# One layer of a hybrid decoder in split single precision: W_down as seven half-size block products

## The chip, the cores and the metric

The kernel runs on one core of a Trainium2 chip. The metric is the device time of one execution in microseconds (us). Beside the times there is a hardware profile of one execution: what each engine did and when. The engines are PE (TensorE, matrix products), ACT (ScalarE), DVE (VectorE), POOL (GpSimd) and SP (SyncE, which here only starts DMAs).

## The reference, cut to what matters

```python
# x: (512, 1024) tokens by features; p: (512, 256); one layer
h = rms_norm(x, g_pre_mix)
q, k, v, cb, cc, cu, ga, gc = split(h @ w_in)             # 8 heads of 64; conv and gates
o = stick_breaking_attention(q, k, v)                     # strictly causal
y_conv = (cb * causal_conv3(cc * cu)) @ w_conv_out
x = x + rms_norm((sigmoid(ga) * (o @ w_attn_out) + sigmoid(gc) * y_conv) @ w_o, g_post_mix)
f = square(relu(rms_norm(x, g_pre_mlp) @ w_up)) @ w_down  # w_up 1024x4096, w_down 4096x1024
x = x + rms_norm(f, g_post_mlp)
x = x + sigmoid(rms_norm(x, g_ple) @ w_ple_gate) * (p @ w_ple_proj)
```

The change is about the second product in the line for f: 512 tokens by 4096 hidden features times W_down.

## The kernel before

Every matrix product is done in split single precision. A value is split into a high part, which ACT copies out in the shorter format float32r, and a low part, which DVE gets as the difference (`split`). `mm3` then issues three matmuls: high by high, high by low, low by high. One matmul is a 128 x 128 stationary tile by 128 x 512 moving columns into a PSUM bank. There are eight banks of 512 columns.

The stages run in this order: norm of x, transposes and v; attention and convolution; the gated mix; W_o with its norms; p @ W_ple_proj; W_up with relu squared; W_down with its norms; the gated per-layer embedding. The order on PE and on SP is the order of the code (`manual_schedule`). The order on ACT, DVE and POOL is made by the framework's scheduler when the kernel is built. Each engine, and each queue of DMAs, works strictly in its order, so one instruction that waits holds all those behind it.

Weights come through `weights` (called by `wcols` and `wrow`): a DMA of 512 KB into one of four `raw` buffers, then two splits of half a tile into a `whi` and a `wlo` tile. The pool `wts` holds five of each. A third pool, `big`, has 16 tiles of 8 KB a partition for activations.

Attention goes over four pairs of heads (the loop over j). For each pair PE makes the scores of head a and of head b (`scores`), then two convolution products (`conv_u`, `conv_b`), then the transposes of head a's weights (`wtrans(wa)`), the next query product, the transposes of head b's weights (`wtrans(wb)`), the next key product, the products with v (`av`, twice), and the next `conv_c`. Inside `scores`, ACT makes two sigmoids, beta and keep; POOL cuts each at the diagonal with `affine_select` (eight of these instructions a head); DVE does a running product over keep (line 304) and a multiplication (line 305), four of each a head. After `wtrans`, DVE makes the low parts `wtl` which `av` reads.

W_down is called as `rows(FF // P, acts, w_down, 4, chain2)`: for each of 32 row blocks k, four token tiles t by two column halves, three matmuls each, accumulating in all eight banks. The last four k are done token tile by token tile, and `chain2(t)` follows each: `residual` squares the sums (ACT), gets the reciprocal root (a `pow` on POOL, line 119, writing `rs`), scales and adds to x (DVE, lines 468 and 469), squares again, `pow` again, and scales (line 475). The result hn2[t] is transposed on PE (`transposed2`, line 127) two token tiles later and split into h3, which the last stage multiplies with W_ple_gate. W_o has the same ending with `chain1`, hn1 and h2.

## Time and profile before

| | |
|---|---|
| times of three runs | 768.0, 768.71, 769.34 us (median 768.71) |
| span of the profiled execution, first to last instruction | 764.4 us |
| PE busy | 756.4 us, 3528 matmuls |
| DVE busy | 388.1 us |
| ACT busy | 301.7 us |
| POOL busy | 49.8 us |
| HBM read, written | 74.99 MB, 2.10 MB |
| granted TensorE clock | 1.000 |

The profiled execution's own time is known as its span; the times of the runs are of other executions, and their median is 4.3 us above the span. A row of the profile names the line of the kernel, the engine, the operation, and out<-in by the names of the tiles; "x236" is a count, and then come busy microseconds, the mean of one in nanoseconds, and the engine's idle time ahead of these instructions with what ended it. Matmuls overlap, so the pitch from one start to the next is shorter than the duration of one. Rows of the timeline start with the start in us and the length in us.

### The profile page before, as it was taken

To read this page: it belongs to the slowest core of one execution; us is meant where nothing else is said; L and a number is where in the kernel's file an instruction comes from. 1 tells how busy PE (TensorE), PEld (TensorE's weight loads), DVE (VectorE), ACT (ScalarE), POOL (GpSimd) and SP (SyncE) were. 2 spreads that over 40 slices of the span, in tenths; PEclk is the share of its full clock that TensorE was granted. 3 is DMA by queue.
4 is the path that set the end of the run, shared out by engine and by line. 5 is a ranking of instruction groups with operands and counts; after the bars stand their busy time and mean duration, and the time that the engine had idled before them with its cause. 6 is when DMAs were issued, how large, how long until landed. Compare 5 with 4: busy or idle time off the path is not lost.

```text
span 764.4 us, 9131 instructions
## 1 busy us (share of the span) xinstructions
PE 756.4 (99%) x3528; PEld 631.9 (83%) x3528; DVE 388.1 (51%) x643; ACT 301.7 (39%) x586; POOL 49.8 (7%) x91
## 2 busy tenths in 40 slices
PE   8999999999999999999999999999999999999997
PEld 6888888888888888888988888888888888888886
DVE  5759797976434345348433333333652543234742
ACT  7654645554333334228323232323631433222511
POOL 1013314040000000001000000000000000000100
PEclk9999999999999999999999999999999999999999
DMA  9512130414634623211633333332323442410011
GB/s 303 163 58 83 55 111 29 131 31 115 193 111 130 200 87 106 83 56 34 187 86 108 86 107 89 104 101 94 110 84 109 138 165 87 161 56 1 0 56 55
DMA packets 91106, 77.66 MB, mean 102 GB/s; under 512 B 2580, under 2 KB 81208, under 8 KB 91064
## 3 DMA queue, kind: packets, MB, share of 16 engines
q1 hardware_dynamic: 91064, 77.10, 32.9%
q8 instruction: 27, 0.44, 0.2%
q14 instruction: 15, 0.12, 0.1%
HBM read 74.99 MB, written 2.10 MB: 101 GB/s over the span
## 4 chain that ended last, share of the span: by engine, by line
PE 98%; ACT 1%; DMA 1%; DVE 0%; issue 0%; SPq 0%; POOL 0%; ACTq 0%
PE ps L83 31%; PE ps L85 31%; PE ps L84 31%; PE ps L334 1%; PE ps L320 1%; PE ps L127 1%; PE ps L293 1%; PE ps L292 1%; DMA xin<-in_x_dram 1%; ACT h1h L197 0%; PE ps L188 0%; ACT vh L61 0%; ACT junk L111 0%; PE ps L433 0%; POOL rs L119 0%
## 5 line engine op out<-in xcount | busy, mean ns | idle before, releaser
L62 DVE TENSOR_TENSOR wlo<-raw,whi 128x512 fp32r<-128x512 f32 x236 | 158.2, 686 | 253.2 <-ACT whi L61 253.0
L61 ACT CAST whi<-raw 128x512 fp32r<-128x512 f32 x236 | 141.5, 623 | 328.1 <-PE ps L84 174.8
L83 PE MATMUL ps<-h1h,whi 128*128 128x512 f32 x288 | 113.0, 392 | 0.0
L85 PE MATMUL ps<-h1h,wlo 128*128 128x512 f32 x288 | 112.3, 390 | 0.0
L84 PE MATMUL ps<-h1l,whi 128*128 128x512 f32 x288 | 112.2, 390 | 0.0
L83 PE MATMUL ps<-h2h,whi 128*128 128x512 f32 (+1 forms) x272 | 102.5, 377 | 0.0
L84 PE MATMUL ps<-h2l,whi 128*128 128x512 f32 (+1 forms) x272 | 102.4, 377 | 0.0
L85 PE MATMUL ps<-h2h,wlo 128*128 128x512 f32 (+1 forms) x272 | 102.4, 377 | 0.0
L83 PE MATMUL ps<-whi,ah 128*128 128x512 f32 x256 | 99.7, 389 | 0.0
L85 PE MATMUL ps<-whi,al 128*128 128x512 f32 x256 | 99.6, 389 | 0.0
L84 PE MATMUL ps<-wlo,ah 128*128 128x512 f32 x256 | 99.6, 389 | 0.0
L85 PEld LDWEIGHTS ps<-h1h,wlo 128*128 128x128 f32 x288 | 54.1, 188 | 11.2
L84 PEld LDWEIGHTS ps<-h1l,whi 128*128 128x128 f32 x288 | 54.1, 188 | 10.9
L83 PEld LDWEIGHTS ps<-h1h,whi 128*128 128x128 f32 x288 | 54.1, 188 | 10.8
L85 PEld LDWEIGHTS ps<-h2h,wlo 128*128 128x128 f32 x272 | 51.2, 188 | 9.4
L84 PEld LDWEIGHTS ps<-h2l,whi 128*128 128x128 f32 x272 | 51.2, 188 | 9.4
L83 PEld LDWEIGHTS ps<-h2h,whi 128*128 128x128 f32 x272 | 51.2, 188 | 9.3
L84 PEld LDWEIGHTS ps<-wlo,ah 128*128 128x128 f32 x256 | 48.1, 188 | 10.0
L85 PEld LDWEIGHTS ps<-whi,al 128*128 128x128 f32 x256 | 48.1, 188 | 9.9
L83 PEld LDWEIGHTS ps<-whi,ah 128*128 128x128 f32 x256 | 48.1, 188 | 9.9
L119 POOL TENSOR_TENSOR rs<-ms,mhalf 128x1 f32<-128x1 f32 x20 | 11.8, 588 | 565.7 <-DVE ms L117 513.5
L301 POOL TENSOR_SCALAR_AFFINE_SELECT beta<-beta 128x128 f32<-128x128 f32 x32 | 26.3, 833 | 107.9 <-ACT beta L295 107.7
(133 smaller groups left out, 1000.3 us busy)
## 6 DMA issues: line engine op xcount, KB each, us to landing
raw<-in_w_in_dram SPq DMA_DIRECT2D x36, 512.0 KB, 3.8
raw<-in_w_up_dram SPq DMA_DIRECT2D x32, 512.0 KB, 4.0
raw<-in_w_down_dram SPq DMA_DIRECT2D x32, 512.0 KB, 3.3
raw<-in_w_o_dram SPq DMA_DIRECT2D x8, 512.0 KB, 3.4
raw<-in_w_ple_gate_dram SPq DMA_DIRECT2D x8, 512.0 KB, 3.3
xin<-in_x_dram SPq DMA_DIRECT2D x4, 512.0 KB, 9.5
vr<-in_w_in_dram SPq DMA_DIRECT2D x4, 512.0 KB, 7.5
raw<-in_w_conv_out_dram SPq DMA_DIRECT2D x8, 256.0 KB, 2.8
```

Of the source, the lines that this page charges most:

```text
L61: nc.scalar.copy(hi, src)
L62: nc.vector.tensor_tensor(lo, src, hi.bitcast(F32), op=ALU.subtract)
L83: nc.tensor.matmul(ps, lh, rh, start=start, stop=False)
L84: nc.tensor.matmul(ps, lh, rl, start=False, stop=False)
L85: nc.tensor.matmul(ps, ll, rh, start=False, stop=stop)
L119: nc.gpsimd.tensor_tensor(r, m, mhalf, op=ALU.pow)
L127: nc.tensor.transpose(ps[:, i * P:(i + 1) * P], hn[g][:, i * P:(i + 1) * P], ident)
L292: nc.tensor.matmul(ps[:, c0:c0 + n], lhs, st[:, 1, 0:n], start=True, stop=False)
L293: nc.tensor.matmul(ps[:, c0:c0 + n], lhs, st[:, 2, 0:n], start=False, stop=True)
L301: nc.gpsimd.affine_select(t_[:, dg], t_[:, dg], pattern=[[-1, P]], compare_op=ALU.is_gt, fill=fill, base=0, channel_multiplier=1)
L320: nc.tensor.transpose(ps[:, c0 + (qb - kb) * P:c0 + (qb - kb + 1) * P], w[:, o:o + P], ident)
L334: nc.tensor.matmul(ps[:, kb * P:S], lhs, wt[i][:, c0:c0 + n], start=(kb == 0 and i == 0), stop=(kb == NT - 1 and i == 1))
```

## The change

Tokens and W_down are each cut in two, and so are W_down's rows and columns and the hidden features. The product of these blocks is then formed from seven half-size block products instead of eight (Strassen's scheme in the variant with common sums). Four products (the first sweep, `t_four` and `s_four`) use four of five sums of W_down's blocks, and three products (the second sweep, `t_three` and `s_three`) use the fifth sum and two blocks of W_down as they are. Each half-size product is, for each of 16 pairs of row blocks j, two token tiles by three matmuls of the same shape as before: 7 x 16 x 2 x 3 = 672 matmuls where 32 x 8 x 3 = 768 stood.

The sums of W_down's blocks are made by `make_sums`, called 16 times: four times in attention, eight times in the mix, once in W_o, once ahead of p @ W_ple_proj and twice in W_up. A call loads two tiles of W_down (512 KB each), does five additions of 128 x 512 on POOL, and its results go to DRAM by three DMAs that `save_sums` issues later on SP. The loads and results take four tiles of the pool `wts`, which is now one ring of 13 tiles for high and low parts alike. The sums of the activations are made on DVE: `half_sums`, eight times in W_up, and three additions in each `s_three`. In the product itself weights come as whole tiles of 128 x 1024 (`load_t`, one copy on ACT and one subtraction on DVE), up to four loads ahead. Finished products are put together on ACT and DVE (`done_four` after the first sweep, `done_three` after the second) in four tiles `cx`, which also come from the ring. In the second sweep the last two i are done product by product: first the two products that finish token tiles 0 and 1, then the one that finishes tiles 2 and 3. `residual1` is `residual` on one 1024-wide tile in SBUF. Four row blocks of W_ple_gate now come through `load_pg` and four through `wrow`; before it was six and two.

```diff
-    wts = ctx.enter_context(tc.tile_pool(name="wts", bufs=5))
+    wts = ctx.enter_context(tc.tile_pool(name="wts", bufs=13))
+    sums = ctx.enter_context(tc.tile_pool(name="sums", bufs=1, space=bass.MemoryType.DRAM))
-        lo = wts.tile(shape, F32R, tag="wlo", name="wlo")
-        hi = wts.tile(shape, F32R, tag="whi", name="whi")
+        lo = wts.tile(shape, F32R, tag="w", name="wlo")
+        hi = wts.tile(shape, F32R, tag="w", name="whi")
...
+    def w4(dt=F32):
+        return wts.tile([P, 2, 512], dt, tag="w", name="w4")
...
+    wd = w_down.rearrange("(h j p) n -> j h p n", h=2, p=P)
+    wsum = [sums.tile([P, 5, 2, 512], F32, name=f"wsum{i}") for i in range(NJ // 2)]
+    unsaved = []
+    def save_sums():
+        while unsaved:
+            dst, src = unsaved.pop(0)
+            nc.sync.dma_start(dst, src)
+    made = iter(range(NJ))
+    def make_sums():
+        save_sums()
+        j = next(made)
+        q = []
+        for h in range(2):
+            t = w4()
+            nc.sync.dma_start(t, wd[j][h].rearrange("p (c n) -> p c n", c=2))
+            q += [t[:, 0], t[:, 1]]
+        dst = wsum[j // 2][:, :, j % 2, :]
+        o = [w4(), w4()]
+        for i, (a, b, op) in enumerate(((1, 3, ALU.subtract), (2, 0, ALU.subtract), (0, 1, ALU.add), (2, 3, ALU.add))):
+            nc.gpsimd.tensor_tensor(o[i // 2][:, i % 2], q[a], q[b], op=op)
+        nc.gpsimd.tensor_tensor(q[0], q[0], q[3], op=ALU.add)
+        unsaved.extend([(dst[:, 0:2], o[0]), (dst[:, 2:4], o[1]), (dst[:, 4], q[0])])
...
     for j in range(4):
         wa = scores(st[0])
         wb = scores(st[1])
+        make_sums()
         y = conv_u(j, ct)
...
         tb = wtrans(wb)
+        save_sums()
         if j < 3:
...
     for j in range(NK):
+        make_sums()
...
         wo2 = weights(two, [P, NK, P])
+        save_sums()
...
         for k in range(nk):
+            if nk == NK and k == 0:
+                make_sums()
+            if nk == NK and k == 3:
+                save_sums()
             wk = wrow(w, k)
...
+    def residual1(xt, c, gpost, gnext):
+        r = rstd_of([c])
+        nc.vector.scalar_tensor_tensor(c, c, r, gpost, op0=ALU.mult, op1=ALU.mult)
+        nc.vector.tensor_tensor(xt, xt, c, op=ALU.add)
+        r2 = rstd_of([xt])
+        nc.vector.scalar_tensor_tensor(c, xt, r2, gnext, op0=ALU.mult, op1=ALU.mult)
+        return [c[:, 0:512], c[:, 512:1024]]
...
+    make_sums()
...
+    def half_sums(g):
+        f = af[g]
+        lo, hi = f[:, :, 0:256], f[:, :, 256:512]
+        if g < 4:
+            nc.vector.tensor_tensor(hi, hi, lo, op=ALU.subtract)
+        else:
+            nc.vector.tensor_tensor(lo, lo, hi, op=ALU.subtract)
     for c in range(2, FF // P):
         if c == 8:
             gpl = gain(g_post_mlp)
             gle = gain(g_ple)
+        if c in (3, 6):
+            make_sums()
+        if c in (2, 5, 8):
+            save_sums()
         relu2(c, proj(wcols(w_up, c * P), hm))
+        if c % 4 == 3:
+            half_sums(c // 4)
...
+    def load_t(keys, src, pool=None):
+        raw = raws.tile([P, 2, 512], F32, tag="raw", name="raw")
+        nc.sync.dma_start(raw, src)
+        lo, hi = (w4(F32R), w4(F32R)) if pool is None else pool
+        split(hi, lo, raw)
+        for u, key in enumerate(keys):
+            tiles[key] = hi[:, u], lo[:, u]
...
+    def t_four(i, pi):
+        load_t([(2 * i + u, pi) for u in range(2)], wsum[i][:, pi])
+    def t_three(i, pi, pool=None):
+        keys = [(2 * i + u, pi) for u in range(2)]
+        if pi == 1:
+            return load_t(keys, wsum[i][:, 4], pool)
+        h = 1 if pi == 0 else 0
+        r0 = h * FF // 2 + i * 2 * P
+        load_t(keys, w_down[r0:r0 + 2 * P, h * 512:h * 512 + 512].rearrange("(k p) n -> p k n", p=P), pool)
+    def s_four(i):
+        g, r = i // 2, 2 * (i % 2)
+        h, l = bigt([P, 2, 2, 512], name="sh"), bigt([P, 2, 2, 512], name="sl")
+        for u in range(2):
+            split(h[:, u], l[:, u], af[g + 4 * u][:, r:r + 2])
+        for v in range(2):
+            for pi, (u, o) in enumerate(((0, 0), (1, 256), (0, 256), (1, 0))):
+                stat[2 * i + v, pi] = h[:, u, v, o:o + 256], l[:, u, v, o:o + 256]
+    def s_three(i):
+        a11, a21 = af[g][:, r:r + 2, 0:256], af[g][:, r:r + 2, 256:512]
+        a12, a22 = af[g + 4][:, r:r + 2, 0:256], af[g + 4][:, r:r + 2, 256:512]
+        nc.vector.tensor_tensor(a11, a11, a22, op=ALU.add)
+        nc.vector.tensor_tensor(a12, a12, a11, op=ALU.add)
+        nc.vector.tensor_tensor(a21, a21, a11, op=ALU.add)
+        h, l = bigt([P, 3, 2, 256], name="sh"), bigt([P, 3, 2, 256], name="sl")
+        for pi, a in enumerate((a12, a11, a21)):
+            split(h[:, pi], l[:, pi], a)
+            for v in range(2):
+                stat[2 * i + v, pi] = h[:, pi, v], l[:, pi, v]
...
+        def mm(self, pi, t, i):
+            if (pi, t) not in self.acc:
+                self.acc[pi, t] = bank()
+            ts = slice(t * P, (t + 1) * P)
+            for j in (2 * i, 2 * i + 1):
+                sh, sl = stat[j, pi]
+                th, tl = tiles[j, pi]
+                mm3(self.acc[pi, t], sh[:, ts], sl[:, ts], th, tl, j == 0, j == NJ - 1)
+    cx = [w4() for _ in range(NT)]
+    def done_four(pi, t, ps):
+        if pi == 0:
+            nc.scalar.copy(cx[t][:, 1], ps)
+        elif pi == 1:
+            nc.scalar.copy(cx[t + 2][:, 0], ps)
+        elif pi == 2:
+            nc.vector.tensor_tensor(cx[t + 2][:, 1], ps, cx[t][:, 1], op=ALU.add)
+        else:
+            nc.vector.tensor_tensor(cx[t][:, 0], ps, cx[t + 2][:, 0], op=ALU.add)
...
+    def chain2(t):
+        c = cx[t].rearrange("p a b -> p (a b)")
+        hn2[t] = residual1(xr2(t), c, gpl, gle)
...
-    rows(FF // P, acts, w_down, 4, chain2)
+    def done_three(pi, t, ps):
+        if pi == 0:
+            nc.vector.tensor_tensor(cx[t][:, 1], cx[t][:, 1], ps, op=ALU.add)
+            nc.vector.tensor_tensor(cx[t][:, 0], cx[t][:, 0], ps, op=ALU.subtract)
+        elif pi == 1:
+            nc.vector.tensor_tensor(cx[t][:, 0], cx[t][:, 0], ps, op=ALU.add)
+            nc.vector.tensor_tensor(cx[t + 2][:, 1], cx[t + 2][:, 1], ps, op=ALU.add)
+            chain2(t)
+        else:
+            nc.vector.tensor_tensor(cx[t + 2][:, 0], cx[t + 2][:, 0], ps, op=ALU.add)
+            nc.vector.tensor_tensor(cx[t + 2][:, 1], cx[t + 2][:, 1], ps, op=ALU.subtract)
+            chain2(t + 2)
...
+    def load_pg(k):
+        wl, wh = bigt([P, 2, D], name="pgl"), bigt([P, 2, D], name="pgh")
...
+    uses = [(0, i, pi, t) for i in range(NI) for pi in range(4) for t in range(2)]
+    uses += [(1, i, pi, t) for i in range(NI - 2) for pi in range(3) for t in range(2)]
+    last = (NI - 2, NI - 1)
+    uses += [(1, i, pi, t) for t in range(2) for pi in range(2) for i in last]
+    uses += [(1, i, 2, t) for t in range(2) for i in last]
...
+        sweeps[w].mm(pi, t, i)
+        if i == NI - 1:
+            (done_four if w == 0 else done_three)(pi, t, sweeps[w].acc[pi, t])
...
+        if w == 1 and i in (2, 4) and (pi, t) == (1, 1):
+            load_pg(i - 2)
+    for k in range(4, NK):
```

Lines ahead of the change's insertions have moved: the low-part subtraction is now line 64, the `affine_select` line 333, the `pow` line 124, the sums lines 293 and 294.

The first place is POOL in attention. Of the eight selects of head a's and the eight of head b's scores, these rows stand before at the passage from head a (its last two) to head b (beta and keep are the two sigmoids):

```order
L301 AFFINE_SELECT beta<-beta 128x128
L301 AFFINE_SELECT keep<-keep 128x128
L301 AFFINE_SELECT beta<-beta 128x128
L301 AFFINE_SELECT keep<-keep 128x128
L301 AFFINE_SELECT beta<-beta 128x128 x2
L301 AFFINE_SELECT keep<-keep 128x128 x2
```

In the changed kernel the same place, with the sums that iteration j + 1 makes (w_981 and w_983 are its two tiles of W_down, w_985 and w_986 its results):

```order
L333 AFFINE_SELECT beta<-beta 128x128
L333 AFFINE_SELECT keep<-keep 128x128
L293 TENSOR_TENSOR w_985<-w_981,w_983 128x512
L333 AFFINE_SELECT beta<-beta 128x128
L293 TENSOR_TENSOR w_985<-w_983,w_981 128x512
L333 AFFINE_SELECT keep<-keep 128x128
L333 AFFINE_SELECT beta<-beta 128x128 x2
L333 AFFINE_SELECT keep<-keep 128x128 x2
L333 AFFINE_SELECT beta<-beta 128x128
L333 AFFINE_SELECT keep<-keep 128x128
L293 TENSOR_TENSOR w_986<-w_981 128x512
L293 TENSOR_TENSOR w_986<-w_983 128x512
```

The first two sums have moved in front of head b's first select of beta and its first select of keep, and the other three (the last, on line 294, is the next row) follow right behind head b's selects; the loops for j = 0, 1 and 2 have the same pattern.

The second place is POOL at the norms that follow W_o. Before, all the `pow` instructions (rs) stand together behind the last selects:

```order
L301 AFFINE_SELECT beta<-beta 128x128 x2
L301 AFFINE_SELECT keep<-keep 128x128 x2
L301 AFFINE_SELECT beta<-beta 128x128
L301 AFFINE_SELECT keep<-keep 128x128
L119 TENSOR_TENSOR rs<-ms,mhalf 128x1 x16
```

Now the fifteenth set of sums, which W_up's loop makes at c = 3, has its place among W_o's eight `pow` instructions:

```order
L124 TENSOR_TENSOR rs<-ms,mhalf 128x1 x7
L293 TENSOR_TENSOR w_3565<-w_3561,w_3563 128x512
L293 TENSOR_TENSOR w_3565<-w_3563,w_3561 128x512
L293 TENSOR_TENSOR w_3566<-w_3561 128x512
L293 TENSOR_TENSOR w_3566<-w_3563 128x512
L294 TENSOR_TENSOR w_3561<-w_3561,w_3563 128x512
L124 TENSOR_TENSOR rs<-ms,mhalf 128x1
```

The five sums stand ahead of the eighth `pow`, which is the second one of token tile 3.

The third place is DVE where W_down ends. Before, the norm of a token tile stands there as follows (ms is the mean square that `pow` takes, gb the gain):

```order
L117 SCALAR_TENSOR_TENSOR ms<-ss 128x1
L468 SCALAR_TENSOR_TENSOR tmp<-ps,rs,gb 128x512 x2
L469 TENSOR_TENSOR xr<-xr,tmp 128x512 x2
L115 TENSOR_SCALAR ms<-ss 128x1
L475 SCALAR_TENSOR_TENSOR tmp<-xr,rs,gb 128x512 x2
```

Now, from the first addition that completes token tile 0 (w_4645 to w_4648 are the four `cx` tiles, ps the banks):

```order
L686 TENSOR_TENSOR w_4645<-w_4645,ps 128x512
L687 TENSOR_TENSOR w_4647<-w_4647,ps 128x512
L64 TENSOR_TENSOR wlo<-raw,whi 128x512
L120 TENSOR_SCALAR ms<-ss 128x1
L64 TENSOR_TENSOR wlo<-raw,whi 128x512
L505 SCALAR_TENSOR_TENSOR w_4645<-w_4645,rs,gb 128x1024
L683 TENSOR_TENSOR w_4646<-w_4646,ps 128x512
L506 TENSOR_TENSOR xr<-xr,w_4645 128x1024
L684 TENSOR_TENSOR w_4646<-w_4646,ps 128x512
L64 TENSOR_TENSOR wlo<-raw,whi 128x512
L120 TENSOR_SCALAR ms<-ss 128x1
L686 TENSOR_TENSOR w_4646<-w_4646,ps 128x512
```

The additions of finished products (lines 683 to 687) and the low parts of W_ple_gate (wlo) now stand between the steps of a token tile's norm.

More of the change, by code (lines that the diff above doesn't have):

```diff
@@ L24 @@
 FF = 4096
+NJ = FF // P // 2
 EPS = 1e-6
@@ new lines, in hybrid_block, with load @@
+    last = (NI - 2, NI - 1)
+    uses += [(1, i, pi, t) for t in range(2) for pi in range(2) for i in last]
+    uses += [(1, i, 2, t) for t in range(2) for i in last]
+    loads = list(dict.fromkeys(u[:3] for u in uses))
+    tail2 = []
+    def load(w, i, pi):
+        if w == 0:
+            t_four(i, pi)
+        elif pi < 2 or i < NI - 2:
+            t_three(i, pi)
+        else:
+            if not tail2:
+                tail2.extend([bigt([P, 4, 512], name="th"), bigt([P, 4, 512], name="tl")])
+            u = 2 * (i - last[0])
+            t_three(i, 2, (tail2[1][:, u:u + 2], tail2[0][:, u:u + 2]))
```

52 lines of the change are left out of this document (30 added, 22 removed).

## The prediction

> **What bounds the kernel now.** I read the engines' busy times first, then the chain that ended last, then the W_down product alone, then two stages that the change touches.
>
> ```profile
> PE 756.4 (99%) x3528; PEld 631.9 (83%) x3528; DVE 388.1 (51%) x643; ACT 301.7 (39%) x586; POOL 49.8 (7%) x91
> PE 98%; ACT 1%; DMA 1%; DVE 0%; issue 0%; SPq 0%; POOL 0%; ACTq 0%
> GB/s 303 163 58 83 55 111 29 131 31 115 193 111 130 200 87 106 83 56 34 187 86 108 86 107 89 104 101 94 110 84 109 138 165 87 161 56 1 0 56 55
> ```
>
> PE is never free: it is 99% of the span and 98% of the chain. So a removed matmul is worth its full pitch, and every new wait of PE costs its full length. The pitch is read from line 83, every third matmul of the product:
>
> ```profile
> L83 PE MATMUL ps<-whi,ah x221: 389/389/389, 539.8 to 689.4; 128*128 128x512 f32 x111
> ```
>
> From the first to the last of these 221 there are 220 x 3 = 660 steps in 149.6 us: 0.2267 us each (the 389 ns of one overlaps its neighbours).
>
> The other engines have unequal room. The rows are stretches of the span with each engine's busy time; the clock column is 1.00 in both:
>
> ```profile
> 89.00:123.00 34.00, 34.00 (x170) 28.77 (x169) 29.12 (x47) 18.79 (x39) 8.92 (x15) 1.00 0.27 79
> 396.00:700.00 304.00, 304.00 (x1343) 251.81 (x1342) 115.64 (x179) 99.70 (x179) 0.55 (x1) 1.00 0.33 102
> ```
>
> From 396 to 700 us (W_up and W_down) DVE works 115.6 of 304 us. In one pair of heads (89 to 123 us) it works 29.1 of 34 us: attention has almost no room on DVE, and four of the sixteen calls of make_sums are put there, with a fifth that the order moves in.
>
> **Step 1, the matmuls.** 768 become 672: 96 x 0.2267 = 21.8 us less. Transposes, shapes and the rest of PE's work are unchanged. Nothing else in the change saves time.
>
> **Step 2, work that I cost at nothing, and its cover.**
>
> ```profile
> L62 DVE TENSOR_TENSOR wlo<-raw,whi 128x512 fp32r<-128x512 f32 x236 | 158.2, 686 | 253.2 <-ACT whi L61 253.0
> L62 DVE TENSOR_TENSOR pgl<-raw,pgh 128x1024 fp32r<-128x1024 f32 x6 | 7.3, 1224 | 19.6 <-ACT pgh L61 16.3 <-PE ps L84 3.3
> L61 ACT CAST whi<-raw 128x512 fp32r<-128x512 f32 x236 | 141.5, 623 | 328.1 <-PE ps L84 174.8 <-PE ps L85 76.4 <-issue 76.4
> L61 ACT CAST pgh<-raw 128x1024 fp32r<-128x1024 f32 x6 | 6.3, 1050 | 18.4 <-DMA raw<-in_w_ple_gate_dram 18.4
> raw<-in_w_down_dram SPq DMA_DIRECT2D x32, 512.0 KB, 3.3
> ```
>
> The two sweeps take PE 672 x 0.2267 = 152.3 us. DVE has there 56 loads and 16 activation tiles at 1.224 (88.1), 24 additions and 24 splits at 0.686 (32.9), four W_ple_gate halves (4.9) and four joins (2.7): 128.6 us, 84% of PE's time, so PE hides it while the lead of up to four loads (4 x 12 matmuls, 10.9 us) lasts; without that cover each late us counts fully. ACT's 72 copies at 1.05 and 24 at 0.623 make 91 us. The DMAs are 56 x 512 KB in 152 us, 193 GB/s; the GB/s row shows 303 moved at the start. Half_sums adds 8 x 1.224 = 9.8 us to DVE in W_up, where it is idle for most of the time. The extra traffic outside, 32 loads of 512 KB and 21 MB of results, stands beside at most 200 GB/s from the second slice on.
>
> SP: save_sums waits until POOL is done, and the next loads queue behind it. In the mix one j is 72 matmuls, 16.3 us; tile load 3.3 plus five sums with waits (7.9, next step) is 11.2 us, and the three weight loads of that j have gone out before the save. The wait is covered until that chain reaches 16.3, with one sum at 2.2 us. The 80 DMAs of the sums and 24 more loads also cost SP their issue, but it has time:
>
> ```profile
> SPq L67 <- DVE wlo L62: 460.4, 104, 9.2
> ```
>
> For 460 us it only waits until DVE has emptied a raw buffer. The ring of 13 is shorter than it looks: a set of sums takes four tiles and cx, at the end, four for good. Nine are left, four pairs of high and low; three pairs ahead of PE are at least 3 x 2.7 us (the second sweep's 12 matmuls a pair), against 3.3 + 1.05 + 1.22 = 5.6 us from a load's issue to its low part. If the ring ran dry each lack would cost its length; I take nothing for it.
>
> **Step 3, GpSimd's sums in attention.** No row shows a 128 x 512 addition on POOL; the nearest is the select.
>
> ```profile
> L301 POOL TENSOR_SCALAR_AFFINE_SELECT beta<-beta x32: 293/887/1208, 53.8 to 166.0; 128x128 f32<-128x128 f32 x32
> 89.39 1.95 POOL L301 TENSOR_SCALAR_AFFINE_SELECT beta<-beta 128x128 f32<-128x128 f32 x2 [0.19 <-ACT beta L295]
> 89.23 1.22 DVE L304 TENSOR_TENSOR_SCAN keep<-keep 128x512 f32<-128x512 f32 x1 [1.27 <-POOL keep L301]
> 93.04 0.61 POOL L301 TENSOR_SCALAR_AFFINE_SELECT beta<-beta 128x128 f32<-128x128 f32 x1
> 93.71 1.94 DVE L304 TENSOR_TENSOR_SCAN keep<-keep 128x256 f32<-128x256 f32 x2
> 110.93 1.62 DVE L62 TENSOR_TENSOR wtl<-ps,wth 128x512 fp32r<-128x512 f32 x3
> 113.81 0.69 DVE L62 TENSOR_TENSOR wlo<-raw,whi 128x512 fp32r<-128x512 f32 x1 [1.26 <-ACT whi L61]
> 113.35 2.48 PE ps L334 x16
> ```
>
> (The last row is a piece of the chain.) A free select takes 0.293 us. Beside DVE's scan, which reads SBUF twice, two selects take 1.95: POOL is held by such a DVE instruction. The reverse, DVE held by POOL, no row shows, since a select is too short for it. I assume it, because a sum is four selects long, with zero as the low end. Price g of one sum: 0.686 (DVE's row, same shape) at the least, 4 x 0.293 = 1.17 by the select's columns, 2.34 if the two operands are read one after the other. I take 1.17.
>
> Where it falls: head b's second scan (the 512-wide one behind 93.71, so at 94.41) needs head b's first keep select. Now two sums stand in front of it: from 93.04, 0.4 wait, g, 0.7 for the DVE instruction held, 0.3 select, 0.3 wait, g, 0.3 select make 95.04 + 2g, so that scan is 0.63 + 2g late = 2.97 us. Three more sums follow among DVE instructions that mostly read SBUF twice; each costs g less some 0.43 that runs beside an instruction reading PSUM: 2.2. DVE is 5.2 us late. None of its rows from 94 to 110 shows idle time, and the next idle time stands ahead of 113.81; so the lateness reaches head b's wtl (110.93, first piece done at 111.6). PE needs that in the second av, 113.35 + 1.24 + 0.2 = 114.8. Slack 3.2, so PE waits 2.0 us, in three passes (j = 0, 1, 2): 6.0 us. In the fourth pass five sums come behind the selects, 3.7 us late where two query subtractions (1.4) are missing: slack 4.6, nothing. Low end 0; with g = 1.35 it is 8.7.
>
> The SBUF page of the Trainium skill ("SBUF — State Buffer", Who interferes with whom) states that a DVE instruction with two SBUF inputs and a GpSimd instruction that reads SBUF shut each other out for a whole instruction, whichever starts first. The trace agrees for POOL held (median 887 against 293 ns); with the rule taken for DVE as well the sum stays as above, without it this step is 0. The page "GPSIMD Engine Reference" (3.1) has 1.96 times DVE's time for a 2048-wide addition; by it, as an estimate, g is 1.34 us and the whole sum would come to 765.5.
>
> **Step 4, the norms behind W_o.**
>
> ```profile
> 355.52 0.93 POOL L119 TENSOR_TENSOR rs<-ms,mhalf 128x1 f32<-128x1 f32 x1 [2.19 <-DVE ms L117]
> 361.03 0.55 POOL L119 TENSOR_TENSOR rs<-ms,mhalf 128x1 f32<-128x1 f32 x1 [4.58 <-DVE ms L115]
> 365.89 0.87 PE ps L127 x8
> ```
>
> Five sums now stand between these two pow. Behind 356.45, five times g + 0.4 end at 364.3, so the last pow is 3.3 us late and hn1[3] comes at 364.3 + 0.55 + 1.4 = 366.3; PE's transposes want it at 365.9. I add 0.5, and 0.5 for the thirteenth and fourteenth sets, which wait for ring tiles that the W_o product frees. 1.0 us; ends 0 and 4.
>
> **Step 5, the end of W_down.** Before:
>
> ```profile
> 696.97 0.19 ACT L111 ACTIVATION_READ_ACCUMULATOR junk<-ps 128x1 f32 x1
> 699.41 1.28 DVE L469 TENSOR_TENSOR xr<-xr,tmp 128x512 f32<-128x512 f32 x2
> 700.79 1.06 ACT L111 ACTIVATE junk<-xr 128x1024 bf16<-128x1024 f32 x1 [3.62 <-DVE xr L469]
> 702.27 0.55 POOL L119 TENSOR_TENSOR rs<-ms,mhalf 128x1 f32<-128x1 f32 x1 [4.22 <-DVE ms L115]
> 702.86 1.41 DVE L475 SCALAR_TENSOR_TENSOR tmp<-xr,rs,gb 128x512 f32<-128x512 f32 x2 [0.73 <-POOL rs L119]
> 707.27 0.87 PE ps L127 x8
> 726.30 0.87 PE ps L127 x8
> ```
>
> Token tile 0's result is there at 704.3, and PE wants it at 707.3. Now call T0 the moment when token tile 0 is complete. From T0 to the transposes of hn2[3], PE has 24 + 12 + 12 + 24 + 24 = 96 matmuls (21.8) and three groups of transposes (2.6): 24.4 us. In DVE's order, from the addition that completes tile 0 to hn2[3], stand 25 instructions of 512 columns (ten of them additions of finished products, eight W_ple_gate low parts, six of h3, one product of the last stage), 12 of 1024 and 8 of one column. Back to back they take 0.60 to 0.69 (two in 1.28), 1.22 and 0.15: 25 x 0.63 + 12 x 1.22 + 8 x 0.15 = 31.6 us, and about 1.0 of waits for pow that nothing fills. DVE is late by 32.6 - 24.4 = 8.2 us, and PE waits that long in the transposes. Most of it has come up by hn2[1]: 15 x 0.63 + 6 x 1.22 + 4 x 0.15 = 17.4 us of DVE work stand ahead of that, and PE would be ready 48 matmuls and one group of transposes, 10.9 + 0.9 = 11.8 us, behind T0. Ends: 5 with 0.60 throughout and no waits, 11 with full durations.
>
> **Sum** against the profiled execution: 764.4 - 21.8 + 6.0 + 1.0 + 8.2 = 757.8 us of span. The median of the runs, 768.71, lies 4.3 above its span, which I keep: 762.1 us.
>
> **Rivals.**
> Almost the full gain: DVE is not held by POOL. Step 3 is then 0 (the late keep select stays under the slack of 3.2) and step 4 is 0.5: 755.6, and 752.4 with step 5 at 5. For it: no row shows DVE held. Against it: half of POOL's beta selects are three times as long as a free one, so something is shared.
> Slower: POOL's addition is slow. Step 3 is 3 x (5g - 3.86), plus 5g - 6.75 from g = 1.35 on, and step 4 grows by 5 per us. At 2.34 that makes 28.5 and 6.9: 790 us. The sum is zero at g = 1.47, 0.30 above my value, so this mechanism decides the sign. For it: two operands, and no row of such an addition. Against it: POOL would have to be over 2.1 times as slow as DVE's 0.686.
> DVE becomes the bound in the sweeps: 128.6 us of work leaves 23.7 of waits. If it reaches only 75% there (in its order, behind late copies) the sweeps take 171.5, 19 us more: 781. Against it: the lead of 10.9 us in the first sweep is nine DVE instructions long, and its order puts most of the second sweep's additions into the first, where 4 x 1.224 + 2 x 1.224 + 3 x 0.686 = 9.4 of each 10.9 us are used, and 3 x 1.224 + 3 x 0.686 = 5.7 of 8.2 in the second.
> No change: steps 3 to 5 near their upper ends (8.7 + 3 + 10) eat 21.7.
>
> **How the numbers follow.** A difference under 0.2% (1.5 us) can't be told from none. My forecast (755.5 to 767): 0.50. Almost the full gain: 0.20. Within 1.5 us of before: 0.10. Slow addition: 0.14. DVE-bound sweeps: 0.06. So faster 0.70, same 0.10, slower 0.20. The range leaves out one in ten at each end: 751 (21.8 saved, step 5 at 5, nothing else) to 775 (g near 1.6, or a sweep 10 us late); the likeliest case's own is 755.5 to 767.
>
> **What would show it.** In the changed trace: matmuls of lines 88 to 90 at the pitch of 0.227 and 96 fewer; POOL's sums at about 1.2 us, longer beside DVE; PE idle ahead of the second av in three passes, some 2 us each, released by DVE; the eighth pow near its transposes; and PE idle of 1 to 5 us ahead of the transposes of cx, 8 in all, with DVE unbroken from T0. Idle PE inside the sweeps, or sums over 1.5 us, would prove me wrong.

## The result, and the profile after

Measured together, the changed kernel takes 778.0 us (median of 4 runs) and the kernel before 768.5: a ratio of 1.0122, 95% interval 1.0108 to 1.0137. It is slower by 9.5 us, where 762.1 and a gain were forecast. The profiled execution of the changed kernel took 777.72 us with a span of 776.0.

The page of the changed kernel, in the same order as before (engine totals, then the chain that ended last):

```profile
PE 745.7 (96%) x3432; PEld 618.4 (80%) x3432; DVE 478.8 (62%) x681; ACT 337.0 (43%) x584; POOL 158.6 (20%) x171
PE 59%; DVE 5%; DMA 3%; POOL 2%; issue 2%; ACT 1%; SPq 0%; ACTq 0%; DVEq 0%; POOLq 0%
```

The 96 matmuls are gone, but PE is busy for 96% of a longer span, and only 10.7 us less than before instead of 21.8. PE was 98% of the chain and is 59%: others now decide when it runs. The chain of waits, for PE (us in total, times, the longest):

```profile
PE ps L88 <- DVE tmp L393: 11.8, 4, 3.8
PE ps L132 <- DVE ms L120: 2.8, 1, 2.8
PE ps L132 <- DVE w L508: 2.4, 1, 2.4
PE ps L89 <- DVE wlo L64: 2.4, 1, 2.4
```

The first row is attention, the other three are the end of W_down. All four wait for DVE.

Outside W_down PE's instructions stand in the same order in both kernels, so the start of each in one trace less its start in the other shows where PE fell behind. From the start times:

| stretch | forecast | measured |
|---|---|---|
| head, up to attention | 0 | +1.0 |
| attention, passes 0 to 3 (step 3) | 2.0, 2.0, 2.0, 0 | +4.5, +3.5, +3.5, +6.0; 17.6 in all |
| mix and W_o (step 4) | +1.0 | +1.4 and +1.8 |
| W_up and W_down to token tile 0 (steps 1 and 2) | -21.8 | -21.8 |
| end of W_down (step 5) | +8.2 | +11.6 |
| span | -6.6 | +11.6 |

Of the 96 saved matmuls 72 lie ahead of the point where token tile 0 is complete (16.3 us by the start times); the other 24 are counted there too, at the pitch of 0.2267 us. The saving came in full. The costs were forecast at 15.2 us and are 33.4.

**Attention.** Timeline of the changed kernel in pass 1, POOL, DVE and PE (start, length; in brackets the idle time ahead and what ended it):

```profile
98.17 1.59 POOL L293 TENSOR_TENSOR w<-w,w 128x512 f32<-128x512 f32 x1
100.03 1.66 POOL L293 TENSOR_TENSOR w<-w,w 128x512 f32<-128x512 f32 x1
101.97 1.29 DVE L336 TENSOR_TENSOR_SCAN keep<-keep 128x512 f32<-128x512 f32 x1 [1.37 <-POOL keep L333]
105.70 2.87 POOL L293 TENSOR_TENSOR w<-w 128x512 f32<-128x512 f32 x2
109.15 1.33 DVE L337 TENSOR_TENSOR beta<-beta,keep 128x255 f32<-128x255 f32 x1
110.52 0.69 DVE L383 TENSOR_TENSOR tmp<-tmp,ps 128x512 f32<-128x512 f32 x1
115.37 0.68 DVE L393 TENSOR_TENSOR tmp<-ps,tmp 128x512 f32<-128x512 f32 x1
116.11 0.50 PE L88 MATMUL ps<-h1h,whi 128*128 128x512 f32 x1 [2.68 <-DVE tmp L393]
```

Two sums ahead of head b's first keep select make DVE's scan wait. Against the kernel before (scan at 94.41; DVE's first scan of the pass is 5.1 us later here) it is 2.4 us late, DVE's instruction on line 383 is 5.1 us late, and conv_b's product on line 393 is 6.1 late. PE then stands still for 2.68 us: the key product needs a PSUM bank, and the next in turn is the one that line 393 still reads.

Pass 3 has two sets among its selects, the first two of the mix. The five sums of one stand ahead of head a's selects. POOL waits 2.9 us among them for an earlier set's save, and DVE's first scan, at 173.69 us, is 2.6 us late (PE starts this pass 12.6 us later than before). The other five stand behind head b's selects and make it 6.8 us by line 383.

How DVE is held shows in the groups by shape, before (line 305) and after (line 337):

```profile
L305 DVE TENSOR_TENSOR beta<-beta,keep 128x255 f32<-128x255 f32 x8 | 3.4, 425 | 0.0
L305 DVE TENSOR_TENSOR beta<-beta,keep 128x127 f32<-128x127 f32 x8 | 2.6, 325 | 0.0
```

```profile
L337 DVE TENSOR_TENSOR beta<-beta,keep 128x127 f32<-128x127 f32 x8 | 10.0, 1245 | 0.0
L337 DVE TENSOR_TENSOR beta<-beta,keep 128x255 f32<-128x255 f32 x8 | 7.3, 908 | 0.1
```

The same products take 2 to 4 times as long. With the 256-wide scans (724 ns before, 1273 after) that is 8 x (0.92 + 0.48 + 0.55) = 15.6 us of DVE's time, 3.9 a pass.

**The clock.** The stretches around pass 0's gap (PE busy, its instructions, granted clock, DMA share, GB/s):

```profile
74.00:76.00 2.00, 0.32 (x3) 1.00 0.51 146
76.00:78.00 2.00, 1.05 (x4) 0.90 0.81 239
78.00:80.00 2.00, 2.00 (x6) 0.50 0.00 0
80.00:82.00 2.00, 2.00 (x8) 0.75 0.00 0
82.00:84.00 2.00, 2.00 (x11) 1.00 0.00 0
```

A gap is paid twice. Some microseconds after PE fell idle the clock is halved: worked out from the three clock values under 1.00, for 0.4 + 2.0 + 1.0 = 3.4 us, in which PE does 1.7 us less work. Net it cost less here: pass 0 lost 4.5 us and passes 1 and 2, at full clock, 3.5, for there PE loses another 0.6 us at av, where head b's low parts are late. The same stands behind pass 3's gap of 3.84 us and twice in the end of W_down, but not behind the gaps of passes 1 and 2 (2.68 and 2.67). The mean clock is 0.990 where it was 1.000. The Trainium skill ("TensorE: Matmul & The Clock Gate", Part 1) says that PE's activity is watched in free-running windows of 3.4 us and that an idle window halves the clock until a busy one has passed. The 3.4 us agree, and so does the grid: every change of the clock in these traces lies on steps of 3.41 us, whose phase differs from run to run. The window need not be wholly idle: a gap of 2.63 us that fell into one window was enough here, and the last section has the count.

**The sweeps** (PE, PEld, DVE, ACT, POOL busy) and **the end:**

```profile
560.00:700.00 140.00, 140.00 (x619) 115.96 (x618) 113.86 (x123) 84.07 (x97) 0.00 (x0) 1.00 0.63 196
706.00:740.00 34.00, 26.34 (x116) 21.40 (x115) 30.22 (x44) 15.51 (x28) 5.34 (x7) 0.90 0.02 9
```

In the sweeps PE has no gap with DVE at 81%. In the end DVE is busy for 30.2 of 34 us, PE for 26.3.

### The profile page after: what moved, and what is told of

It is laid out like the page before. It is cut to its first block, busy times and chain, and to the rows that moved or that the text cites. A ratio compares the mean times of both kernels' runs of the same rounds, so it can differ in the third digit from the quotient of the medians.

```text
span 776.0 us, 9363 instructions
## 1 busy us (share of the span) xinstructions
PE 745.7 (96%) x3432; PEld 618.4 (80%) x3432; DVE 478.8 (62%) x681; ACT 337.0 (43%) x584; POOL 158.6 (20%) x171
## 4 chain that ended last, share of the span: by engine, by line
PE 59%; DVE 5%; DMA 3%; POOL 2%; issue 2%; ACT 1%; SPq 0%; ACTq 0%; DVEq 0%; POOLq 0%
PE ps L89 20%; PE ps L88 20%; PE ps L90 20%; DMA raw<-in_w_up_dram 1%; POOL rs L124 1%; POOL w L293 1%; DMA raw<-in_w_down_dram 1%; DMA raw<-in_w_ple_gate_dram 1%; DVE w L508 0%; DVE w L505 0%; DMA w<-in_w_down_dram 0%; DVE w L64 0%; DVE xr L506 0%; ACT whi L63 0%; DVE tmp L523 0%
## 5 line engine op out<-in xcount | busy, mean ns | idle before, releaser
L64 DVE TENSOR_TENSOR wlo<-raw,whi 128x512 fp32r<-128x512 f32 x176 | 119.6, 712 | 154.8 <-POOL w L294 69.3
L63 ACT CAST whi<-raw 128x512 fp32r<-128x512 f32 x176 | 100.9, 621 | 109.6 <-PE ps L90 29.4
L88 PE MATMUL ps<-h1h,whi 128*128 128x512 f32 x288 | 114.6, 398 | 11.8 <-DVE tmp L393 11.8
L124 POOL TENSOR_TENSOR rs<-ms,mhalf 128x1 f32<-128x1 f32 x20 | 13.6, 681 | 362.4 <-DVE ms L120 354.5
L64 DVE TENSOR_TENSOR w<-raw,w 128x1024 fp32r<-128x1024 f32 x54 | 65.8, 1221 | 32.8 <-issue 19.1
L88 PE MATMUL ps<-w,sh 128*128 128x512 f32 x216 | 84.0, 389 | 0.0
L89 PE MATMUL ps<-w,sh 128*128 128x512 f32 x216 | 84.0, 389 | 0.0
L90 PE MATMUL ps<-w,sl 128*128 128x512 f32 x216 | 84.0, 389 | 0.0
L293 POOL TENSOR_TENSOR w<-w,w 128x512 f32<-128x512 f32 x32 | 43.6, 1379 | 142.3 <-DMA w<-in_w_down_dram 142.3
L63 ACT CAST w<-raw 128x1024 fp32r<-128x1024 f32 x54 | 56.5, 1052 | 27.8 <-PE ps L90 24.8
L558 ACT ACTIVATE tmp<-ps 128x512 f32<-128x512 f32 x32 | 19.1, 597 | 107.1 <-PE ps L90 107.1
```

What stands on the lines that cost most here:

```text
L63: nc.scalar.copy(hi, src)
L64: nc.vector.tensor_tensor(lo, src, hi.bitcast(F32), op=ALU.subtract)
L88: nc.tensor.matmul(ps, lh, rh, start=start, stop=False)
L89: nc.tensor.matmul(ps, lh, rl, start=False, stop=False)
L90: nc.tensor.matmul(ps, ll, rh, start=False, stop=stop)
L124: nc.gpsimd.tensor_tensor(r, m, mhalf, op=ALU.pow)
```

## Experiments

Each time stands beside runs of the kernel before on the same chip (768.2 to 768.5 us); all edits but one are to the changed kernel.

**1. Attention's four sets made in W_up.**

```diff
-        make_sums()            # in attention, behind scores(st[1])
-        save_sums()            # in attention, behind wtrans(wb)
...
-        if c in (3, 6):
+        if c in (3, 6, 9, 12, 15, 18):
             make_sums()
-        if c in (2, 5, 8):
+        if c in (2, 5, 8, 11, 14, 17, 20):
             save_sums()
```

> The changed kernel, with the four sets of sums of attention made in W_up instead (at c = 9, 12, 15, 18, saved at c = 11, 14, 17, 20); the sets of the mix, of W_o and the rest stay. Of the built order POOL then has no sum in the passes j = 0, 1 and 2; the first two sets of the mix still stand in the pass j = 3. Theory (sums among the selects make DVE late, and PE waits for it at the bank that conv_b's product frees): matmul by matmul against the kernel before, passes 0, 1 and 2 lost 4.5, 3.0 and 3.5 us and pass 3 lost 6.3. The first three go, 11 us, and the fourth stays: 778.0 - 11 = 767 us, PE idle ahead of the key product (line 88) in pass 3 alone, and W_up without a gap. Rival (the price of the sums goes where they go: ring tiles, DMA traffic and DVE's delay by GpSimd are as dear in W_up): 775 to 778 us, with gaps in W_up. Rival 2 (the gaps come from the ring of 13 or from the weights' order, not from the sums): the gaps in passes 0 to 2 stay, 778 us.

767.6 us (ratio 0.9996, 0.9976 to 1.0015). PE has no gap in passes 0 to 2 nor in W_up, and pass 3 keeps gaps of 1.8 and 3.8 us: both rivals fall. Moved sums cost nothing there.

**2. The kernel before with attention's four sets and the ring of 13 tiles that they need.**

```diff
-    wts = ctx.enter_context(tc.tile_pool(name="wts", bufs=5))
+    wts = ctx.enter_context(tc.tile_pool(name="wts", bufs=13))
...
+        make_sums()            # behind scores(st[1]), in the kernel before
...
+        save_sums()            # behind wtrans(wb)
```

> The kernel before, with the four sets of sums of attention added and nothing else of the change but the ring of 13 tiles that they need (loads, additions on GpSimd, saves to DRAM that nothing reads). Theory: passes 0, 1 and 2 lose 4.5, 3.0 and 3.5 us as in the changed kernel and pass 3, which has no set of the mix here, nothing: 768.5 + 11 = 779.5 us, a gap of 2.6 us ahead of three key products, and the granted clock at half for some 3 us behind at least one of them. Rival (the gaps need the rest of the change, say the mix's sets or other orders): within 2 us of 768.5. By the prediction's own step 3 it would be 768.5 + 6.0 = 774.5.

783.0 us (1.0184, 1.0157 to 1.0212), slower than the whole change. The three gaps are there, 2.65, 2.66 and 2.66 us, pass 3 is free, and the start times show passes 0 to 2 losing 4.0, 4.5 and 4.3 us, 12.9 in place of 11 (another 3.8 us of this execution lie in the head): the clock is halved behind the second and the third gap, where in the changed kernel it was the first.

**3. Memsets in place of attention's sums.**

```diff
+        if j < 4:
+            for i in range(5):
+                nc.gpsimd.memset(ts[i % 2], 0.0)
...
+            return
```

> The changed kernel, with the five sums of each of attention's four sets replaced by five memsets of 128x1024 on GpSimd into the set's two tiles; loads, saves and all other sets stay. The saved values of these four sets are not sums of W_down. A memset writes SBUF and reads nothing; by the row of the 128x128 memset at the start (0.204 us, and 0.098 for one column) it should take about 0.95 us. The built order puts three of the five ahead of head a's selects, one ahead of head b's first keep select and one behind it. Theory (DVE is held by GpSimd's reading of SBUF): DVE's products of line 337 beside a memset keep their free length (0.41 us for 255 columns, 1.33 beside a sum), DVE is 1 us late at most, passes 0 to 2 have no gap and pass 3 keeps its loss from the mix's two sets: 778.0 - 11 = 767 us. Rival (any long GpSimd instruction holds DVE, or the loads, saves and ring tiles make the gaps): lengthened products on line 337, gaps of 1 us and more in passes 0 to 2, 770 to 778 us.

766.1 us (0.9980, 0.9963 to 0.9997), no gap in passes 0 to 2. The memsets on POOL (shortest, median, longest in ns), then DVE's products by shape:

```profile
L294 POOL MEMSET w<- x20: 948/954/1224, 22.2 to 130.5; 128x1024 f32 x20
```

```profile
L343 DVE TENSOR_TENSOR beta<-beta,keep 128x255 f32<-128x255 f32 x8 | 4.6, 571 | 0.1
L343 DVE TENSOR_TENSOR beta<-beta,keep 128x127 f32<-128x127 f32 x8 | 3.4, 428 | 0.0
```

The products are near their old length; in experiment 1, where only pass 3 has sums, as here, they take 564 and 462 ns. So loads, saves and ring tiles cost nothing, and a GpSimd instruction that only writes was not seen to hold DVE. Since the memsets also stand elsewhere among the selects, the run alone doesn't divide the delay of the select from the hold; the lengthened products do. "SBUF — State Buffer" of the Trainium skill (Who interferes with whom) excepts an instruction that only writes, as seen here.

**4. All five sums behind head b's selects.**

```diff
-        make_sums()
+        with tc.issue_after(sel.ins):   # sel: head b's last select
+            make_sums()
...
```

> The changed kernel, with the set of pass j held back on GpSimd until head b's last select of that pass, so that no sum stands in front of a select: all five stand behind (in pass 3 the mix's first two sets follow them). Theory (DVE is held by each sum, whatever its place): three sums behind the selects cost DVE 2.7 us in the changed kernel, 0.9 each, so five cost 4.5; with a slack of some 3 us PE waits 1 to 2 us in passes 0 to 2 and about 4 in pass 3; the clock may stay up at the shorter gaps: 766 to 772 us. Rival (only the order counts: a sum delays a select and nothing else): no gaps in passes 0 to 2, and 760 to 762 us.

825.1 us (1.074, 1.0719 to 1.076): neither the theory's time nor the rival's. Waits of SP, ACT and PE:

```profile
SPq L278 <- POOL w L293: 223.6, 32, 38.2
ACT whi L63 <- DMA raw<-in_w_in_dram: 82.2, 16, 15.8
PE ps L90 <- DVE wlo L64: 34.3, 4, 8.9
```

SP had run most of a pass ahead and now stood in save_sums for sums that come later; the weights behind it in its queue came late, and PE waited 8.4 to 8.9 us a pass for their low parts and 3.7 for their high parts. The experiment says nothing on its question, but prices a wait that the prediction had costed at nothing.

**5. Filling PE's gaps.** In the first kernel 24 idle transposes stood behind head b's copies, in the second, whose edit is shown, 22 ahead of them.

```diff
+            for _ in range(fill if group == (2,) else 0):
+                nc.tensor.transpose(ps[:, 384:512], ident, ident)
             split(wh[:, base:base + n], wl[:, base:base + n], ps[:, 0:n])
```

> The changed kernel, with 24 transposes of the identity (some 2.4 us of PE) into unused columns of head b's last bank ahead of each key product, at the place where PE sits idle; no result uses them. Theory (PE waits there anyway, and the clock falls because PE is idle): the fillers cost nothing, the granted clock stays at 1.00 through attention, and the two stretches at 0.50 behind passes 0 and 3 (1.5 and 1.4 us lost) go: 778.0 - 3 = 775 us, the gaps under 0.5 us apart from the fourth (about 1.4). Rival (the lower clock has another cause, such as the power that PE and the other engines draw together, or the state of the run): the clock still falls to 0.50, 778 us. Rival 2 (DVE and ACT see the fillers as contention, or the fillers are longer than the gap): 779 to 782 us.

825.8 us (1.0751, 1.0726 to 1.0776). Writing to the bank, they waited for DVE's wtl that read it (45.0 us in four waits), so PE was held longer than by the gap: a miss of the experiment.

> The changed kernel, with 22 transposes of the identity (some 2.3 us of PE) directly behind head b's last transposes, into unused columns of the same bank and ahead of its copies; no result uses them. In the first filler kernel they stood behind the copies and waited for DVE, which made the gaps 11 us; here they wait for nothing. Theory (the clock falls because PE is idle for 2.7 us): PE idle in attention is under 0.6 us in passes 0 to 2 and 1.5 in pass 3, the granted clock stays at 1.00 through attention, and 1.5 to 1.7 us go for each stretch at half clock that the changed kernel has there (two in its profile): 775 us, or 778 where DVE's copies, which now start 2.3 us later, make head b's wtl late. Rival (the clock falls for another reason): stretches at 0.50 in attention stay.

777.5 us (1.0117, 1.0097 to 1.0137). Attention's gaps at the bank shrink from 11.8 to 2.2 us in all, and the clock stays up where it was halved:

```profile
76.00:78.00 2.00, 1.77 (x13) 1.00 0.85 248
78.00:80.00 2.00, 2.00 (x11) 1.00 0.00 0
```

Idle PE halves the clock, as the theory has it. But little of it is kept. By start times PE reaches the av of pass 0 1.5 us earlier than in the changed kernel, waits there for head b's low parts, which come no sooner, and is 0.4 us earlier at the scores of pass 1; behind pass 3 it is 1.5 us earlier, and in the mix that is lost: at 206 to 211 us, where PE waits twice for 0.8 us, the clock is now halved once, and the norms of W_o wait 1.6 us more.

**6. The second norm taken off the way to the transposes.**

```diff
-        r2 = rstd_of([xt])
-        nc.vector.scalar_tensor_tensor(c, xt, r2, gnext, op0=ALU.mult, op1=ALU.mult)
-        return [c[:, 0:512], c[:, 512:1024]]
+        return [xt[:, 0:512], xt[:, 512:1024]], rstd_of([xt])
...
-            nc.scalar.activation(sg, ps, AF.Sigmoid)
+            nc.scalar.activation(sg, ps, AF.Sigmoid, scale=r2[t])
```

> The changed kernel, with the second norm of W_down's end taken off DVE: hn2[t] is the residual xr itself, the gain g_ple is multiplied into W_ple_gate's rows when they are split (the same number of instructions), and the reciprocal root r2 is applied as the scale of the last stage's sigmoid. Four DVE instructions of 1.22 us and four waits for pow are gone from the way to the transposes. Theory (the end is bound by DVE's order, 32.6 us against PE's 24.4 from the completion of token tile 0 on): DVE's list falls by 4.9 us and the waits of about 1.0, so PE waits some 2 to 3 us in place of 7.7, and with gaps under 2 us the clock does not fall there (3.4 us lost now): 778.0 - 8.5 = 769.5 us. Rival (the end waits for something else, W_ple_gate's loads or ACT's squares and copies): under 2 us of gain, 776 to 778.

The gain g_ple goes into W_ple_gate's rows when they are split. 773.4 us (1.0070, 1.0044 to 1.0097): 4.6 us of the 8.5. By start times the end itself gains 6.1; this execution loses 1.1 us more in the head and 0.6 more in attention. One gap stays, with a halved clock behind it:

```profile
PE ps L132 <- DVE xr L507: 3.2, 1, 3.2
```

It is ahead of hn2[1]'s transposes, only 24 matmuls and one group of transposes behind the completion of token tile 1. DVE's rows from 707.6 to 719.5 us show no idle time, so its order still sets this wait; hn2[0]'s transposes wait no longer.

**7. The transposes of hn2 later in PE's order.**

```diff
-        if t > 1:
-            transposed2(h3, hn2[t - 2], t - 2)
...
+        if (w, i, pi, t) == (1, NI - 2, 2, 1):
+            transposed2(h3, hn2[0], 0)
...
-        if t == 1:
-            transposed2(h3, hn2[3], 3)
...
-            if t == 0 and cs.start == 0:
-                transposed2(h3, hn2[2], 2)
+            if (t, cs.start) in ((0, 0), (0, 512), (1, 0)):
+                n2 = 1 + 2 * t + cs.start // 512
+                transposed2(h3, hn2[n2], n2)
```

> The changed kernel, with the four groups of transposes of hn2 moved later in PE's order and nothing else: hn2[0]'s between the last two six-matmul blocks of W_down, hn2[1]'s behind the first half of the last stage's token tile 0, hn2[2]'s behind its second half, hn2[3]'s behind the first half of token tile 1. Theory (DVE's list from the completion of tile 0 on sets when each hn2 is there; PE has 24 to 72 more matmuls of the last stage to do meanwhile): gaps of about 1 us ahead of hn2[0] and 1.6 ahead of hn2[3] in place of 7.7 in all, no fall of the clock: 778.0 - 8 = 770 us. Rival (the end is bound by DVE's sum of work up to the last result, which the order can't change): 776 to 778.

776.3 us (1.0100, 1.0073 to 1.0126), 1.8 us better. By start times the end gains 4.2, half of what was expected (the head of that execution lost 3.5 us more). The clock stays up in the end, but the waits move to the low parts of W_ple_gate and of h3, which stand in DVE's list too, 6.3 us for 7.7:

```profile
PE ps L89 <- DVE wlo L64: 3.4, 2, 2.0
PE ps L90 <- DVE h3l L64: 2.0, 1, 2.0
PE ps L132 <- DVE w L508: 0.9, 1, 0.9
```

The rival is nearer: the end is bound by DVE's work, and an order of PE's alone mostly shifts the wait.

**8. The product without the sums.** The sums are left out; the sweeps multiply blocks of W_down in their place.

```diff
-        load_t([(2 * i + u, pi) for u in range(2)], wsum[i][:, pi])
+        h, r0 = pi % 2, (pi // 2) * FF // 2 + i * 2 * P
+        load_t([(2 * i + u, pi) for u in range(2)],
+               w_down[r0:r0 + 2 * P, h * 512:h * 512 + 512].rearrange("(k p) n -> p k n", p=P))
...
-        if pi == 1:
-            return load_t(keys, wsum[i][:, 4], pool)
-        h = 1 if pi == 0 else 0
+        h = 1 if pi < 2 else 0
```

> The changed kernel without make_sums and save_sums: the five sums are left out, and the sweeps load blocks of W_down themselves in their place (56 loads of the same size, from the input tensor in place of the saved sums). It shows the two sweeps and the end by themselves, without what the sums cost. Theory (the losses add up: sums in attention 17.6, mix and W_o 3.1, the end 11.6, sweeps 0): 768.5 - 21.8 + 11.6 = 758.3 us, no gap in attention, mix and sweeps, the end's gaps and stretches at half clock as in the changed kernel. Rival (part of the sums' price is in the sweeps, through DRAM or the ring; or the order of the other engines shifts when the sums go, so that losses come back elsewhere): outside of 756 to 761 us.

756.2 us (0.9848, 0.9831 to 0.9865). By start times 0.5 us is lost before the sweeps, most of it in the head, W_down gains 21.8 up to token tile 0, and the end loses 10.2. The losses add up.

**9. A version with all of it.** No sums in attention, edits 6 and 7, and the sets of W_up two or three column tiles apart (`best`) or three (`best2`).

```diff
+    UPS = (4, 6, 9, 11, 14, 16, 19, 21, 24, 26)        # best; 6 sets in the mix
+    UPS = (7, 10, 13, 16, 19, 22, 25, 28, 31)          # best2; 6 in the mix, 1 in W_o
```

> The changed kernel, with no sums in attention: six sets in the mix (j = 2 to 7), none in W_o, ten in W_up (c = 4, 6, 9, 11, 14, 16, 19, 21, 24, 26); with the second norm's scale in the sigmoid (as in the run late_scale) and with the transposes of hn2 in the later places (as in the run late_turns). Theory: the three losses (attention 17.6 us, mix and W_o 3.1, end 11.6, from the comparison matmul by matmul) go but for about 2 us, and the 21.8 us of the matmuls come through: 768.5 - 21.8 + 2 = 749 us; no stretch of the clock under 1.00 behind attention. Rival (ten sets in W_up cost there, by DVE held or by 270 GB/s of traffic): gaps in W_up, 752 to 760 us.

765.2 us (0.9964, 0.9943 to 0.9985), where 749 was expected. Attention is free of gaps, but in W_up PE waits 7.3 us for copies of weights. SP's and PE's rows for W_up (396 to 560 us) say why:

```profile
SPq L279 <- POOL w L294: 70.8, 16, 7.8
PE ps L88 <- ACT whi L63: 7.3, 3, 3.1
```

> As the run best, with the sets of W_up farther apart: six sets in the mix (j = 2 to 7), one in W_o (k = 0), nine in W_up every third column tile (c = 7, 10, ..., 31). In best three gaps stood in W_up, 1.5 to 3.1 us, where PE waited for a copy of a weight (ACT whi), and with the clock they cost 11 us; there two sets in a row were two column tiles apart (10.9 us of PE), about as long as a set's chain of load, five additions of 1.29 us and save, so that SP stood in the save and the weights behind it came late. Theory: at three tiles (16.3 us), as in sums_in_up, W_up has no gap, and 765 - 11 = 754 us. Rival (the tenfold traffic of sums makes the weights late, or the last set's save at c = 31 holds the first loads of the sweeps): gaps in W_up or at the first sweep's start, 757 to 765 us.

752.9 us (0.9805, 0.9790 to 0.9820): 2.0% faster than before, 25 us faster than the change as it was made, and within 1.1 us of the theory. The page and all that PE waits for from 190 to 690 us:

```profile
PE 739.5 (98%) x3432; PEld 617.3 (82%) x3432; DVE 453.8 (60%) x677; ACT 339.3 (45%) x584; POOL 152.5 (20%) x171
```

```profile
PE ps L89 <- DVE oyl L64: 0.7, 1, 0.7
```

By start times the end still loses 6.1 us in this execution, with two gaps of 1.7 and 2.0 us and a halved clock.

## Why the prediction was wrong

**Step 1** was right: 21.8 us, with the sums and without them.

**Step 2** held: no gap in the sweeps, the ring and the traffic cost nothing (experiments 3 and 8). The cover for save_sums on SP was real but thin: when the sums come later, or their sets stand two column tiles apart, SP's wait is the bound (experiments 4 and 9).

**Step 3** is where it failed, 17.6 us for 6.0. The mechanism was right: DVE is held by a sum, and PE waits for DVE. DVE's lateness at the end of head b's chain, predicted at 5.2 us, was 5.1, and that is partly luck: 2.97 + 2.2 was predicted, 2.4 + 2.7 measured, and a sum took 1.29 us alone and about 1.6 beside DVE instead of 1.17. Three things were missed. First the place: the lateness was followed to head b's wtl and the second av with a slack of 3.2 us, but PE meets it earlier, at the bank that conv_b's product on line 393 has to free for the key product. That made 2.63 to 2.68 us of 2.0, and another 0.6 us at av in passes 1 and 2. Second, pass 3 was costed at nothing: only the five sums behind its selects were counted, not the five ahead of them, and it lost most, 3.84 us of gap and 6.0 in all. In experiment 2, whose pass 3 has no sums, it is free. Third, the clock: no row of before showed a gap within the work, so none showed that the clock falls, and no term was set for it. In attention it took 1.7 us from PE in pass 0, of which 0.4 (experiment 5) to 1.0 (against passes 1 and 2) counted, and 1.5 in pass 3. The four gaps are 11.8 of the 17.6; the rest is the clock, 0.3 us for the restart of PE behind each gap, and the waits at av.

**Step 4** was 3.2 us for 1.0. The five sums do stand ahead of the eighth pow, as said, and there PE waits 0.6 and 0.5 us. The mix was not in the forecast: 1.4 us at its first product, which waits for attention's late low parts (oyl).

**Step 5** was right in its mechanism and its gaps (7.7 us for 8.2, DVE nearly unbroken; 5.2 of them ahead of transposes and 2.4 at W_ple_gate's low parts) and short by the clock, twice 1.7 us. Experiment 6 shows that less work on DVE takes the gaps away, experiment 7 that a later place in PE's order mostly does not.

**The rivals.** None of them was this outcome. Almost the full gain falls, since DVE is held, and so do DVE-bound sweeps, since PE has no gap there. The slow addition had a break-even of 1.47 us for one sum, with 1.29 alone and 1.6 in place: near it, but it named the wrong price of a gap. Its formula 3 x (5g - 3.86) gives 12.4 us at 1.6, near the 11.6 measured for passes 0 to 2, the clock included; its term for pass 3, 5g - 6.75, gives 1.3 us for 6.0. No change had added steps 3 to 5 near their upper ends to 21.7 us; those ends had no place for the clock or for pass 3. The time lies 3 us above the wide range (751 to 775) and 11 above that of the likeliest case, and the change is slower where 0.70 stood on faster.

**The median** was taken 4.3 us above the span. In the changed kernel's executions the time is 1.7 us above the span, in later ones of the kernel before mostly 1.7 to 1.8 and at most 3.2; the rest goes with the clock, which the profiled execution of before had at 1.000, while later ones have, for example, 0.995 (span 767.5) and 0.999 (764.0). So the median was missed by 15.9 us and the span by 18.2: that the median came nearer is luck.

## What to carry to other kernels

Where the bound engine has no gap, price a new wait by its length and by what the clock does after it, and look for the first resource at which the lateness is met: here a PSUM bank in turn came before the operand. An addition on GpSimd is not free beside DVE instructions that read SBUF twice: it belongs where DVE has room, and far enough apart that the queue that saves its result never waits for it. A scale by token can pass a matrix product and be given to the activation behind it; at the end of a stage that shortens the chain and takes work off DVE.

## What was not expected of the hardware

A gap of 2.63 us on PE was enough for 3.4 us at half clock. Of twelve gaps of 2.63 to 2.69 us in passes 0 to 2 of four kernels (the changed one and experiments 2, 6 and 7) six were followed by a halved clock and six were not. What divides them is where they fall on the grid of 3.41 us that the clock's changes lie on: the six had 2.2 to 2.6 us of idle time in one window, the others at most 1.9 in any. In all thirteen traces, behind the first 20 us and at full clock, each of the 32 windows with 2.0 us of idle time or more is followed by one at half clock, and of the rest only one is (1.5 us, the two waits in the mix of experiment 5). The head of the program, where PE has gaps of 0.3 to 2.2 us, differs by up to 4.7 us between executions, with a mean clock of 0.94 to 1.00 in the first 60 us. GpSimd's addition of 128x512 took 1.29 us alone and up to 1.80 beside DVE, where a 128x127 product on DVE took 1.25 us on average for 0.33; beside memsets of twice that size the product took 0.43 on average, with the sums of pass 3 still in it.
